# An SBUF offset: 128 bytes left free at the right end, and the S5 decays moved out of the constants

## The chip, the cores and the metric

The kernel runs on one core of a Trainium2 chip. The metric is the device time of one execution in microseconds (us). Before the change three runs gave 2323.28, 2323.66 and 2326.3 us, so the median is 2323.66 us. The profile was taken from one further execution, which has its own time.

The engines are named as in the profile: PE is the matrix engine, PEld its loading of the stationary operand, DVE the vector engine, ACT the scalar engine, POOL is GpSimd, SP issues most of the transfers. SBUF is the on-chip memory from which PE reads both of its operands; an address in it is a byte offset within each of 128 partitions.

## The reference

A residual trunk of two layers on 1024 positions of width 1024, all in float32. Layer 0 mixes positions with an S5 state-space mixer and a gated linear unit, layer 1 with a gated short convolution. Each mixer is followed by a dense feed-forward network (FFN) of hidden width 2816 and by a gated per-layer embedding (PLE). Cut to what matters:

```python
for i in range(DEPTH):
    hn = rmsnorm(h, norm_mix_g[i])
    mix = s5_mixer(hn, ...) if i % 2 == 0 else shortconv_mixer(hn, ...)
    h = h + mix
    h = h + swiglu_ffn(rmsnorm(h, norm_ffn_g[i]), ffn_w_in[i], ffn_w_out[i])
    gate = sigmoid(rmsnorm(h, norm_ple_g[i]) @ ple_w_gate[i])
    h = h + gate * (p[i] @ ple_w_up[i])
return rmsnorm(h, final_norm_g)
```

## The kernel before

**How a product is made.** Every float32 matrix operand is split into two float32r parts, a high and a low one (`split`, L86: a cast on ACT, L87, and a subtraction on DVE, L88). `mm3` (L121) then adds three products into PSUM: high times high (L122), high times low (L123), low times high (L124). Each is one PE matmul with a stationary operand of 128 partitions by 128 columns and a moving operand of 128 by 512. PE loads a stationary operand anew for each of them. The program has 8712 such full-width matmuls behind the S5 part's own small ones, and they run in long rows one behind another.

**Where the operands lie.** A stack of pools grows from the left end of SBUF and another from the right end. On the left lie the constants (pool `const`), then `ulow` (the activations, or room for weights), the residual `h`, and the pools of the stage: `ws` (weights of the input products), `w8` (shown as `w`, weights of the output products). On the right lie `rawp` (four buffers of 4 KB for what transfers bring in, `raw`; the hidden activations come in there under the name `ch`) and, behind the S5 part, `uhigh` (48 KB, activations or weights). Inside these tiles every matmul operand begins at a multiple of 512 bytes from the tile's start. So an operand's address modulo 512 is that of its tile.

**Which pairs PE reads.** The profile writes a matmul as out<-moving,stationary. Seven pairs make up the full-width float32r products behind the S5 part:

| moving, stationary | stage | matmuls | ends of SBUF |
|---|---|---|---|
| ulow, ws | input products of both FFNs and the convolution | 2688 | left, left |
| uhigh, ws | the same stages | 2016 | right, left |
| ulow, ch | output products of both FFNs and the convolution | 1344 | left, right |
| w, ch | the same | 576 | left, right |
| uhigh, ch | output products of both FFNs | 576 | right, right |
| uhigh, ulow | half of the gated linear unit and of each PLE gate | 768 | right, left |
| w, ulow | the other half | 744 | left, left |

The input products use a seven-product block scheme (`block_product`): of its seven products the first four read `ulow`, the last three `uhigh`, always against `ws`. The output products run in groups of hidden tiles whose weights lie in `ulow`, `uhigh` or `w8`, always with `ch` as the stationary operand.

**What sets the order.** The program is written engine by engine through a scheduler that takes the order of the text, priorities and a model of times; each engine then runs its own list in order. The S5 part's decay table `r8` (256 bytes per partition) is read by the scan on DVE (L981, L982) and by nothing else.

Of the kernel before, what the change touches and what calls it, by code (L numbers as in the profile page):

```python
# [9 lines left out]
F32 = mybir.dt.float32  # L10
# [7 lines left out]

P = 128
MAGIC = 12582912.0  # L20


@with_exitstack
def trunk(
# [17 lines left out]
    NG, NP = s5_a_re.shape[1], s5_a_re.shape[2]  # L42
# [5 lines left out]
    const = ctx.enter_context(tc.tile_pool(name="const", bufs=1))  # L48
# [562 lines left out]
    for tl, v in ((sgnA, 1.0), (sgnN, -1.0)):  # L611
        V.memset(tl[R0], v)
        V.memset(tl[R1], -v)
    r8 = const.tile([P, NG], F32, name="r8")
    rstd = const.tile([P, T], F32, name="rstd")

    rawp = ctx.enter_context(tc.tile_pool(name="rawp", bufs=1, side="right"))
    gen = tc.alloc_tile_pool(name="s5g", bufs=1, side="right")
    st = tc.alloc_tile_pool(name="s5t", bufs=1, side="right")

    def small(shape=(P, NG), dt=F32):
        return st.tile(list(shape), dt, name="sm", tag="sm", bufs=28)

    def ts(o, a, s1, op0, s2=None, op1=None):
        if op1 is None:
            V.tensor_scalar(o, a, s1, None, op0)
        else:
            V.tensor_scalar(o, a, s1, s2, op0, op1)
        return o
# [5 lines left out]
    def stt(o, a, s, b, op0, op1):  # L635
        V.scalar_tensor_tensor(o, a, s, b, op0, op1)
        return o

    def exp_to(o, a, shape):
        n = small(shape)  # L640
        ts(n, a, 1.4426950408889634, ALU.mult, MAGIC, ALU.add)
        ts(n, n, -MAGIC, ALU.add, 129.0, ALU.min)
        ts(n, n, -127.0, ALU.max)
# [86 lines left out]
    kq = small()  # L730
    ts(kq, ang, 2.0 / math.pi, ALU.mult, MAGIC, ALU.add)
    ts(kq, kq, -MAGIC, ALU.add)
    r = small()
# [3 lines left out]
    m4 = small()  # L737
    ts(m4, kq, 0.25, ALU.mult, MAGIC, ALU.add)
    ts(m4, m4, -MAGIC, ALU.add)
    stt(m4, m4, -4.0, kq, ALU.mult, ALU.add)  # L740
# [423 lines left out]
```

## Time and profile before

| | us |
|---|---|
| median of three runs | 2323.66 |
| the profiled execution | 2323.06 |
| its span, first to last instruction | 2321.3 |
| PE busy (matmuls) | 2240.0 (96% of the span) |
| PE loading stationary operands | 1832.0 (79%) |
| DVE busy | 1331.0 (57%) |
| ACT busy | 765.3 (33%) |
| POOL busy | 161.8 (7%) |

How to read it: a matmul's record lasts longer than its turn on PE, since one begins while the one before still drains. The record of a full-width matmul is some 0.39 us long, while the next one starts 0.23 us after it. So the pace of PE is read from the distance between starts, which the timeline gives, and not from the mean length of a record. The page's chain of waits gives PE 91% of the span; the mean granted clock of PE is 0.987 of the full one.

### The profile page before, as it was taken

What the parts mean: (1) busy time and instruction counts of PE and PEld (TensorE: products, weight loads), DVE (VectorE), ACT (ScalarE), POOL (GpSimd) and SP (SyncE); (2) the same over time, 40 slices, a digit from 0 to 9 for tenths busy, and PEclk for the clock granted to TensorE, in tenths of its full rate; (3) what the DMA queues carried; (4) which work ended last, traced back from release to release, by engine and by line L of the source; (5) the groups of instructions that cost most, each with busy time, mean ns of one, the idle gap of its engine ahead of it and who ended that gap; (6) DMA issues with size and microseconds to landing.
All of it is one profiled execution on the core that took longest, in us unless ns stands there. A gap on an engine that the chain in (4) does not pass through costs nothing.

```text
span 2321.3 us, 27094 instructions
## 1 busy us (share of the span) xinstructions
PE 2240.0 (96%) x10253; PEld 1832.0 (79%) x10253; DVE 1331.0 (57%) x2244; ACT 765.3 (33%) x1449; POOL 161.8 (7%) x268
## 2 busy tenths in 40 slices
PE   6987999899999999999989999979999999999998
PEld 5776887688888888888868888868888888888887
DVE  7885325866666642224488776486666666222444
ACT  6554223433333320013343332253333333100232
POOL 2110001000000000000010000010000000000000
PEclk9999999999999999999989999989999999999999
DMA  7656201333333365433232234544333334643323
GB/s 245 149 138 150 70 19 69 103 109 109 109 109 109 109 227 181 149 119 114 89 111 84 92 94 152 192 131 118 109 109 109 109 109 141 231 163 123 127 87 109
DMA packets 212978, 288.87 MB, mean 124 GB/s; under 512 B 21360, under 2 KB 152432, under 8 KB 212848
## 3 DMA queue, kind: packets, MB, share of 16 engines
q1 hardware_dynamic: 191520, 212.63, 29.3%
q0 software_dynamic: 20928, 74.47, 10.4%
q8 instruction: 80, 1.31, 0.2%
q14 instruction: 50, 0.41, 0.1%
q10 hardware_dynamic: 400, 0.04, 0.0%
HBM read 190.93 MB, written 79.69 MB: 117 GB/s over the span
## 4 chain that ended last, share of the span: by engine, by line
PE 91%; DVE 4%; DMA 3%; ACT 1%; SPq 1%; issue 1%; POOL 0%; DVEq 0%; POOLq 0%; ACTq 0%
PE psmm L122 29%; PE psmm L124 29%; PE psmm L123 29%; PE pstr L185 1%; PE pstr L997 1%; DVE W L632 1%; DMA raw<-in_ffn_w_in_dram 1%; PE pstr L998 0%; PE pstr L999 0%; PE pstr L931 0%; DMA tw<-tmp 0%; DVE gv L982 0%; DVE tmp L632 0%; DVE xn L177 0%; PE pstu L122 0%
## 5 line engine op out<-in xcount | busy, mean ns | idle before, releaser
L122 PE MATMUL psmm<-ulow,ws 128*128 128x512 f32 x896 | 351.8, 394 | 5.7 <-ACT ws L87 3.1
L123 PE MATMUL psmm<-ulow,ws 128*128 128x512 f32 x896 | 351.5, 393 | 2.5 <-DVE ulow L88 2.5
L124 PE MATMUL psmm<-ulow,ws 128*128 128x512 f32 x896 | 351.4, 393 | 2.0 <-DVE ws L88 2.0
L124 PE MATMUL psmm<-uhigh,ws 128*128 128x512 f32 x672 | 265.3, 395 | 0.0
L122 PE MATMUL psmm<-uhigh,ws 128*128 128x512 f32 x672 | 265.0, 395 | 0.0
L123 PE MATMUL psmm<-uhigh,ws 128*128 128x512 f32 x672 | 264.9, 394 | 0.0
L409 DVE TENSOR_TENSOR h<-psmm,h 128x512 f32<-128x512 f32 x128 | 88.3, 690 | 234.4 <-PE psmm L124 234.4
L88 DVE TENSOR_TENSOR ws<-raw,ws 128x512 fp32r<-128x512 f32 x224 | 153.6, 688 | 115.1 <-ACT ws L87 115.0
L87 ACT CAST ws<-raw 128x512 fp32r<-128x512 f32 x224 | 137.8, 619 | 208.7 <-PE psmm L124 201.9
L122 PEld LDWEIGHTS psmm<-ulow,ws 128*128 128x128 f32 x896 | 169.6, 189 | 43.6 <-ACT ws L87 4.2
L123 PEld LDWEIGHTS psmm<-ulow,ws 128*128 128x128 f32 x896 | 169.6, 189 | 39.7 <-DVE ulow L88 3.5
L124 PEld LDWEIGHTS psmm<-ulow,ws 128*128 128x128 f32 x896 | 169.5, 189 | 39.1 <-DVE ws L88 3.0
L123 PE MATMUL psmm<-ulow,ch 128*128 128x512 f32 x448 | 177.2, 396 | 0.0
L122 PE MATMUL psmm<-ulow,ch 128*128 128x512 f32 x448 | 176.9, 395 | 0.0
L124 PE MATMUL psmm<-ulow,ch 128*128 128x512 f32 x448 | 176.9, 395 | 0.0
L87 ACT CAST ws<-st 128x512 fp32r<-128x512 f32 x168 | 104.2, 620 | 211.9 <-PE psmm L124 192.1
L123 PEld LDWEIGHTS psmm<-uhigh,ws 128*128 128x128 f32 x672 | 126.2, 188 | 30.3
L124 PEld LDWEIGHTS psmm<-uhigh,ws 128*128 128x128 f32 x672 | 126.1, 188 | 30.3
L122 PEld LDWEIGHTS psmm<-uhigh,ws 128*128 128x128 f32 x672 | 126.2, 188 | 29.0
L370 POOL DMA_DIRECT2D hid<-hs x104 | 78.1, 754 | 917.6 <-DVE hs L88 908.7
L140 ACT ACTIVATE junk<-h 128x512 bf16<-128x512 f32 (+1 forms) x113 | 64.1, 567 | 207.6 <-DVE h L409 122.8
L88 DVE TENSOR_TENSOR ws<-st,ws 128x512 fp32r<-128x512 f32 x168 | 115.2, 686 | 1.3 <-ACT ws L87 1.2
(241 smaller groups left out, 3997.9 us busy)
## 6 DMA issues: line engine op xcount, KB each, us to landing
hid<-hs POOLq DMA_DIRECT2D x104, 512.0 KB, 4.3
ch<-hid SPq DMA_DIRECT2D x96, 512.0 KB, 3.8
raw<-in_ffn_w_in_dram SPq DMA_DIRECT2D x88, 512.0 KB, 4.4
raw<-in_ffn_w_out_dram SPq DMA_DIRECT2D x44, 512.0 KB, 4.0
hd<-h POOLq DMA_DIRECT2D x24, 512.0 KB, 2.9
h<-hd SPq DMA_DIRECT2D x24, 512.0 KB, 5.8
raw<-in_conv_w_in_dram SPq DMA_DIRECT2D x24, 512.0 KB, 3.9
up<-ev SPq DMA_DIRECT2D x32, 256.0 KB, 3.2
```

Source lines behind the costliest of these rows:

```text
L87: A.copy(hi, src)
L88: V.tensor_tensor(lo, src, hi.bitcast(F32), ALU.subtract)
L122: PE.matmul(ps, ahi, bhi, start=start, stop=False, skip_group_check=more)
L123: PE.matmul(ps, ahi, blo, start=False, stop=False, skip_group_check=more)
L124: PE.matmul(ps, alo, bhi, start=False, stop=stop, skip_group_check=more)
L140: done["square"] = A.activation(junk[:, cs], h[t][:, cs], AF.Square, scale=1.0 / math.sqrt(D), accum_out=ms).ins
L185: PE.transpose(pt[:, c * P:(c + 1) * P], xn[:, kt * P:(kt + 1) * P], ident)
L370: nc.gpsimd.dma_start(out=hid[ht // 4][half * HT:(half + 1) * HT, :, ht % 4].rearrange("t p l j -> p t l j"), in_=hs.bitcast(F32))
L409: done["sum"] = V.tensor_tensor(h[t][:, cs], ps[nb], h[t][:, cs], ALU.add).ins
L632: V.tensor_tensor(o, a, b, op)
L997: PE.matmul(o, Us[b][:, g, :], Ms[b][:, g, :], start=True, stop=False)
```

## The change

No instruction is added, removed or moved: every engine's list, with its waits, is the same as before, name for name. Only addresses change. A tile of 32 float32 words (128 bytes per partition) is laid at the right end of SBUF and never written or read, so everything on the right begins 128 bytes lower. And `r8` leaves the constants at the left end for the S5 part's own pool on the right, so everything to the left that lies behind the constants begins 256 bytes lower.

```diff
+EDGE = 32
...
-    r8 = const.tile([P, NG], F32, name="r8")
     rstd = const.tile([P, T], F32, name="rstd")
 
+    edge = ctx.enter_context(tc.tile_pool(name="edge", bufs=1, side="right"))
+    edge.tile([P, EDGE], F32, name="edge")
     rawp = ctx.enter_context(tc.tile_pool(name="rawp", bufs=1, side="right"))
     gen = tc.alloc_tile_pool(name="s5g", bufs=1, side="right")
+    r8 = gen.tile([P, NG], F32, name="r8")
     st = tc.alloc_tile_pool(name="s5t", bufs=1, side="right")
```

What the built programs give as the tiles' first bytes:

| tile | end | before | modulo 512 | after | modulo 512 |
|---|---|---|---|---|---|
| ulow | left | 18016 | 96 | 17760 | 352 |
| ws, first buffer | left | 83552 | 96 | 83296 | 352 |
| w (w8), first buffer | left | 116320 | 96 | 116064 | 352 |
| uhigh | right | 163808 | 480 | 163680 | 352 |
| raw and ch, first buffer | right | 212960 | 480 | 212832 | 352 |
| ws, end of the last buffer | left | 128608 | | 128352 | |
| w, end of the last buffer | left | 149088 | | 148832 | |
| r8 | | 17632 | 224 | 174688 | 96 |
| ident (transposes) | left | 16512 | 128 | 16512 | 128 |

Before, a left and a right tile differ by 128 (or 384) modulo 512; after, by nothing. Modulo 128 no full-width matmul operand moves.

## The prediction

> **What bounds the kernel now.** I began with the page: busy time by engine, then the chain of work that ended last.
>
> ```profile
> PE 2240.0 (96%) x10253; PEld 1832.0 (79%) x10253; DVE 1331.0 (57%) x2244; ACT 765.3 (33%) x1449; POOL 161.8 (7%) x268
> ...
> PE 91%; DVE 4%; DMA 3%; ACT 1%; SPq 1%; issue 1%; POOL 0%; DVEq 0%; POOLq 0%; ACTq 0%
> ```
>
> PE is busy nearly always, and 91% of the chain is its own. Whether it is short of work inside a stage is seen in the busy time by stretches; the columns are the stretch, its length, busy us and count for PE, PEld, DVE, ACT and POOL, then the granted clock, the DMA share and GB/s.
>
> ```profile
> 400.00:500.00 100.00, 90.88 (x394) 73.11 (x393) 78.58 (x135) 43.89 (x80) 6.53 (x10) 0.95 0.36 108
> ...
> 500.00:800.00 300.00, 300.00 (x1308) 245.26 (x1307) 197.73 (x312) 108.12 (x188) 23.95 (x32) 1.00 0.39 112
> 860.00:1080.00 220.00, 220.00 (x970) 179.14 (x969) 62.53 (x84) 30.40 (x49) 3.27 (x6) 1.00 0.43 146
> 1300.00:1400.00 100.00, 100.00 (x437) 81.72 (x436) 73.39 (x111) 33.62 (x54) 7.76 (x16) 1.00 0.31 96
> 1600.00:1900.00 300.00, 300.00 (x1308) 245.08 (x1307) 197.72 (x311) 107.03 (x187) 22.46 (x30) 1.00 0.38 109
> 2000.00:2180.00 180.00, 180.00 (x789) 146.60 (x788) 47.38 (x60) 21.98 (x31) 1.10 (x2) 1.00 0.44 150
> ```
>
> Inside the FFN and convolution stages PE never stops: 300.00 of 300.00 us, at the full clock. The next engine, DVE, has work for 197.73 us of 300. Idle time stands at the borders of stages, as in the first row, where the clock falls too. So in the stages the time is the number of matmuls times the distance between two starts, and I looked next at whether this distance is the same for all pairs of operands. First the numbers of matmuls, from the groups kept apart by shape (one of the three lines of `mm3` each, out<-moving,stationary, then busy us and the mean ns of a record):
>
> ```profile
> L122 PE MATMUL psmm<-ulow,ws 128*128 128x512 f32 x896 | 351.8, 394 | 5.7 <-ACT ws L87 3.1 <-ACT ulow L87 1.9 <-ACT s L348 0.7
> L122 PE MATMUL psmm<-uhigh,ws 128*128 128x512 f32 x672 | 265.0, 395 | 0.0
> L122 PE MATMUL psmm<-ulow,ch 128*128 128x512 f32 x448 | 176.9, 395 | 0.0
> L122 PE MATMUL psmm<-uhigh,ulow 128*128 128x512 f32 x256 | 100.9, 397 | 0.6 <-ACT uhigh L87 0.6
> L122 PE MATMUL psmm<-w,ch 128*128 128x512 f32 x192 | 76.2, 397 | 0.0
> L122 PE MATMUL psmm<-uhigh,ch 128*128 128x512 f32 x192 | 74.8, 390 | 0.0
> ```
>
> The records' means differ little. The starts, from PE's timeline, differ more. For each pair I show the first and the last row of a stretch within one run of that pair, on the same line of `mm3`; the first column is the start in us.
>
> ```profile
> 1707.44 0.39 PE L124 MATMUL psmm<-ulow,ws 128*128 128x512 f32 x1
> ...
> 1714.24 0.39 PE L124 MATMUL psmm<-ulow,ws 128*128 128x512 f32 x1
> 1714.46 0.40 PE L122 MATMUL psmm<-uhigh,ws 128*128 128x512 f32 x1
> ...
> 1719.36 0.39 PE L122 MATMUL psmm<-uhigh,ws 128*128 128x512 f32 x1
> ```
> ```profile
> 2000.04 0.39 PE L124 MATMUL psmm<-ulow,ch 128*128 128x512 f32 x1
> ...
> 2012.64 0.39 PE L124 MATMUL psmm<-ulow,ch 128*128 128x512 f32 x1
> ```
> ```profile
> 1000.58 0.39 PE L122 MATMUL psmm<-uhigh,ch 128*128 128x512 f32 x1
> ...
> 1005.34 0.39 PE L122 MATMUL psmm<-uhigh,ch 128*128 128x512 f32 x1
> ```
> ```profile
> 300.57 0.39 PE L122 MATMUL psmm<-w,ulow 128*128 128x512 f32 x1
> ...
> 307.37 0.39 PE L122 MATMUL psmm<-w,ulow 128*128 128x512 f32 x1
> ```
> ```profile
> 2189.98 0.39 PE L122 MATMUL psmm<-w,ch 128*128 128x512 f32 x1
> ...
> 2191.38 0.39 PE L122 MATMUL psmm<-ulow,ch 128*128 128x512 f32 x1
> ```
> ```profile
> 2231.16 0.39 PE L124 MATMUL psmm<-uhigh,ulow 128*128 128x512 f32 x1
> ...
> 2234.64 0.39 PE L124 MATMUL psmm<-uhigh,ulow 128*128 128x512 f32 x1
> ```
>
> With the matmuls in between counted:
> - both operands at one end: ulow,ws 6.80 us / 30 = 226.7 ns; uhigh,ch 4.76 / 21 = 226.7; w,ulow 6.80 / 30 = 226.7.
> - one operand at each end: uhigh,ws 4.90 / 21 = 233.3; ulow,ch 12.60 / 54 = 233.3; w,ch 1.40 / 6 = 233.3; uhigh,ulow 3.48 / 15 = 232.0.
>
> All of it at clock 1.00, and the first two stretches follow each other within 12 us. The pairs of one end start at one offset modulo 512 (96 and 96, or 480 and 480), those of two ends do not (96 and 480). Neither the tile, nor its role as moving or stationary operand, nor the stage sorts them: uhigh is fast against ch and slow against ws, ulow fast against ws and slow against ch.
>
> **The change, part by part.** No instruction comes, goes or moves, and no wait; so no queue and no wait is passed by another, and only what an address does to a duration can change.
>
> *The full-width products.* After the change all seven pairs begin at 352, so each should step as the pairs of one end do now. The offset 352 itself has no row; 96 and 480, which differ in both address bits that the change moves, have the same 226.7 ns, so I take that. Matmuls of both ends are three times the rows' counts:
> - uhigh,ws 3 × 672 = 2016, by 6.6 ns: 13.3 us
> - ulow,ch 3 × 448 = 1344, by 6.6: 8.9 us
> - w,ch 3 × 192 = 576, by 6.6: 3.8 us
> - uhigh,ulow 3 × 256 = 768, by 5.3: 4.1 us
>
> That is 30.1 us. All of it lies on the path, since PE is full in these stages.
>
> *What is taken off.* A faster PE asks its suppliers sooner: the FFN's input stages give DVE 300 / 1.013 = 296 us for the same 198 us of work, which is still far from full. ACT and DVE wait for PE there, not the other way about, as the waits by engine say (us in total, times, the longest):
>
> ```profile
> ACT ws L87 <- PE psmm L124: 394.0, 216, 4.0
> DVE h L409 <- PE psmm L124: 234.4, 108, 7.5
> PE psmm L122 <- ACT ws L87: 3.1, 3, 1.3
> ```
>
> At the starts of stages PE waits for chains of DVE, ACT and transfers that keep their length. There some products of two ends run while PE is not the bound. If at each of six borders it is one block's 36, that is 36 × 6.6 ns = 0.24 us, 1.4 us in all; if it is all of them in 100 us around it (436 × 3/7 = 187, 1.2 us), 7.4 us. I take 1.5, since the waits that end PE's idle time are few and short in the row above, and keep 0 and 7.
>
> *The other engines.* ACT, DVE and the transfers read and write the shifted tiles too. The nearest rows are the subtraction in `split`, with its two SBUF inputs at two offsets (raw at 480, ws at 96) and at one (st and ws, both at 96):
>
> ```profile
> L88 DVE TENSOR_TENSOR ws<-raw,ws 128x512 fp32r<-128x512 f32 x224 | 153.6, 688 | 115.1 <-ACT ws L87 115.0
> L88 DVE TENSOR_TENSOR ws<-st,ws 128x512 fp32r<-128x512 f32 x168 | 115.2, 686 | 1.3 <-ACT ws L87 1.2
> ```
>
> 2 ns in 688, and behind PE's work. I take nothing; if DVE's 4% of the chain (93 us, mostly the S5 part) moved by that share, it would be 0.3 us either way. The transposes against ident, which begins at 128, have two offsets before (480 or 96) and after (352).
>
> ```profile
> L185 PE MATMUL pstr<-ident,xn 128*128 128x128 f32 x264 | 37.7, 284 | 12.7 <-DVE xn L177 12.7
> L963 PE MATMUL pb<-U,wbt 128*128 128x128 f32 x128 | 17.3, 286 | 2.2 <-ACT wbt L914 2.2
> ```
>
> The S5 part's product U,wbt (left and right) becomes a pair of one offset; at the same 3% (6.6 of 226.7) its 17.3 us would give 0.5 us, and the transposes' 37.7 us could lose or gain 1.1 us. I take zero for both, with ±1.6 us.
>
> *A change of pair.* The first three steps of a one-end run behind a two-end run are longer, 0.69 us / 3 = 230 ns:
>
> ```profile
> 1720.06 0.39 PE L122 MATMUL psmm<-ulow,ws 128*128 128x512 f32 x1
> ...
> 1720.75 0.39 PE L122 MATMUL psmm<-ulow,ws 128*128 128x512 f32 x1
> ```
>
> If that is the delay of the run ahead being caught up, it goes too: 3 × 3.3 = 10 ns, once in each of the 56 blocks of the input stages (2688 / 48) 0.6 us, and with the output stages at most some 2 us. I leave it out of the sum and in the range.
>
> *Sum.* 30.1 − 1.5 = 28.6 us. The profiled execution's 2323.06 us (span 2321.3 and 1.8 around it) becomes 2294.5; it stands 0.6 us below the median of the runs, so the forecast for the median is 2295 us, 1.2% less.
>
> **A rule against it.** The rows say that two reads by PE disturb each other by some 6.6 ns a matmul according to their addresses. The Trainium skill, "SBUF — State Buffer", section "Who interferes with whom", says the contrary: PE has two read ports, one for the moving operand and one for loading the stationary one, independent of each other, and PE never waits on anyone; by it an address could not matter, and the time would stay at 2323.7. The trace disagrees, with 233.3 against 226.7 ns under one clock; the time that the rule gives is the second rival's, and its chance is in that one.
>
> **The rivals.**
> 1. *The gain is eaten by the suppliers.* In the input stages PE would meet transfers and DVE earlier. For it: DVE is at 73.39 of 100 us in the convolution (1300:1400). Against: it is not at 100 anywhere in the rows. If the gain of uhigh,ws were all lost, 13.3 us, the time is 2308.
> 2. *It is the end of SBUF, not the offset.* In the trace the two always go together: every slow pair has one operand at each end. Then nothing changes, and the change does not do what its words say: 2323.7. Against it: distance does not sort the pairs, since ulow (from 18016) with w (up to 149088) is fast though they lie up to 131 KB apart, while uhigh (from 163808) and the last ws buffer (up to 128608) are slow 35 KB apart; a border that does it would have to lie just between 149088 and 163808.
> 3. *Slower: PE, now denser, loses clock.* The mechanism is the granted clock in the stages with PE full, 8712 × 226.7 ns = 1975 us. The gain is gone where 1975 × (1/c − 1) = 28.6, at c = 0.986; at 0.97 it costs 61 us and the time is 2295 + 61 = 2356. Against it: the clock is 1.00 in every row with PE full, those with runs of 226.7 ns steps among them, and falls only where PE stops (0.95 in 400:500).
>
> **How the numbers follow.** Forecast 0.82: 2295 us; with the terms left open (0 to 7 us at the borders of stages, ±1.6 us for S5 and transposes, up to 2 us at changes of pair) 2290 to 2302. First rival 0.09, second 0.06, third 0.03. The range is 2289 to 2303, which takes in the smaller losses of the first rival; outside are the rest of it and the other two. A measurement of this kernel can tell 0.2%, 4.6 us, from no change: the forecast and the first rival are faster by more, 0.91; the second is the same, 0.06; slower 0.03.
>
> **What would show it.** Right: PE's starts in uhigh,ws and ulow,ch at 226.7 ns like ulow,ws, all records of these groups near 390 ns, DVE's and ACT's mean times unchanged, FFN input stages shorter by some 5.2 us each (792 × 6.6 ns), their output stages by 5.1 (768 × 6.6). Wrong: pairs of two ends still at 233 ns (second rival); 226.7 ns reached, but rows of PE with less than 300 of 300 us (first); a clock below 1.00 where PE is full (third); or all pairs at some other step, if 352 is not like 96 and 480.

## The result, and the profile after

The changed kernel takes 2295.32 us (median of four runs, 2293.48 to 2295.71) against 2324.06 us (median of four runs, one more than ahead of the prediction): a ratio of 0.9873, 95% interval 0.9856 to 0.989. Its profiled execution takes 2295.08 us with a span of 2293.3, 28.0 us less than before in both. Timed a second time, beside other runs of the kernel before, the ratio was 0.9878 (0.9862 to 0.9895).

The page after the change: busy time by engine, then the chain.

```profile
PE 2212.2 (96%) x10253; PEld 1831.3 (80%) x10253; DVE 1330.9 (58%) x2244; ACT 765.5 (33%) x1449; POOL 162.4 (7%) x268
...
PE 91%; DVE 4%; DMA 3%; SPq 1%; ACT 1%; issue 0%; POOL 0%; DVEq 0%; POOLq 0%; ACTq 0%
```

PE is busy 27.8 us less for the same 10253 records; DVE, ACT and the loading of stationary operands keep their times. The groups by shape (line numbers of the helpers, `mm3` among them, are one higher than before):

```profile
L123 PE MATMUL psmm<-ulow,ws 128*128 128x512 f32 x896 | 352.3, 394 | 5.9 <-ACT ws L88 3.1 <-ACT ulow L88 2.0 <-ACT s L349 0.7
L123 PE MATMUL psmm<-uhigh,ws 128*128 128x512 f32 x672 | 261.2, 389 | 0.0
L123 PE MATMUL psmm<-ulow,ch 128*128 128x512 f32 x448 | 174.5, 389 | 0.0
L123 PE MATMUL psmm<-uhigh,ulow 128*128 128x512 f32 x256 | 99.5, 391 | 0.6 <-ACT uhigh L88 0.6
L123 PE MATMUL psmm<-w,ch 128*128 128x512 f32 x192 | 75.3, 392 | 0.0
```

The records of the pairs of two ends are now 389 to 392 ns long on this line instead of 395 to 397; ulow,ws stays at 394. The pace is read from the starts again. The first rows of the next fence, from PE's timeline, are the first and the last of a run of `uhigh,ws`; the others belong to the first group of output products of the second FFN, one run of 384 matmuls.

```profile
1695.75 0.39 PE L123 MATMUL psmm<-uhigh,ws 128*128 128x512 f32 x1
...
1700.51 0.39 PE L123 MATMUL psmm<-uhigh,ws 128*128 128x512 f32 x1
...
1951.43 0.39 PE L123 MATMUL psmm<-ulow,ch 128*128 128x512 f32 x1
...
2038.24 0.39 PE L125 MATMUL psmm<-ulow,ch 128*128 128x512 f32 x1
```

That is 4.76 us / 21 = 226.7 ns and 86.81 / 383 = 226.7 ns, where it was 233.3 for both pairs. The clock and the fill of PE in the stages, in the columns of the prediction's stretches:

```profile
500.00:800.00 300.00, 300.00 (x1325) 248.43 (x1324) 200.07 (x315) 108.97 (x189) 24.01 (x32) 1.00 0.39 111
1580.00:1880.00 300.00, 300.00 (x1325) 248.42 (x1324) 199.45 (x315) 108.24 (x188) 23.34 (x32) 1.00 0.39 112
```

PE is still full, still at clock 1.00, and does 1325 matmuls in 300 us instead of 1308.

Where the 28.0 us come from, by the first start of each stage's products in the two timelines (us from one stage's first full-width product to the next one's, in the last row to its own last one):

| stage | before | after | less |
|---|---|---|---|
| S5 part, up to the first product behind it | 221.7 | 222.2 | −0.5 |
| gated linear unit | 188.1 | 185.7 | 2.4 |
| FFN input, layer 0 | 434.0 | 430.1 | 3.9 |
| FFN output, layer 0 | 248.7 | 243.9 | 4.8 |
| PLE, layer 0 | 105.8 | 104.9 | 0.9 |
| convolution input | 233.8 | 230.9 | 2.9 |
| convolution output | 115.1 | 112.0 | 3.1 |
| FFN input, layer 1 | 426.5 | 421.8 | 4.7 |
| FFN output, layer 1 | 248.6 | 243.8 | 4.8 |
| PLE, layer 1 | 85.2 | 84.3 | 0.9 |

All stages with these products gain, and the S5 part ahead of them does not.

### The profile page after: what moved, and what is told of

Same layout as the page of the kernel before. It is cut to its first block, busy times and chain, and to the rows that moved or that the text cites. A ratio compares the mean times of both kernels' runs of the same rounds, so it can differ in the third digit from the quotient of the medians.

```text
span 2293.3 us, 27094 instructions
## 1 busy us (share of the span) xinstructions
PE 2212.2 (96%) x10253; PEld 1831.3 (80%) x10253; DVE 1330.9 (58%) x2244; ACT 765.5 (33%) x1449; POOL 162.4 (7%) x268
## 4 chain that ended last, share of the span: by engine, by line
PE 91%; DVE 4%; DMA 3%; SPq 1%; ACT 1%; issue 0%; POOL 0%; DVEq 0%; POOLq 0%; ACTq 0%
PE psmm L123 29%; PE psmm L125 29%; PE psmm L124 29%; PE pstr L186 1%; DVE gv L985 1%; PE pstr L1000 1%; DVE W L635 1%; PE pstr L1001 1%; PE pstr L1002 1%; DMA tw<-tmp 0%; DMA raw<-in_ffn_w_in_dram 0%; PE pstr L934 0%; DMA W<-W 0%; DVE tmp L635 0%; DMA h<-in_x_dram 0%
## 5 line engine op out<-in xcount | busy, mean ns | idle before, releaser
L124 PE MATMUL psmm<-uhigh,ws 128*128 128x512 f32 x672 | 261.4, 389 | 0.0
L123 PE MATMUL psmm<-uhigh,ws 128*128 128x512 f32 x672 | 261.2, 389 | 0.0
L125 PE MATMUL psmm<-uhigh,ws 128*128 128x512 f32 x672 | 261.2, 389 | 0.0
L124 PE MATMUL psmm<-ulow,ch 128*128 128x512 f32 x448 | 174.6, 390 | 0.0
L123 PE MATMUL psmm<-ulow,ch 128*128 128x512 f32 x448 | 174.5, 389 | 0.0
L125 PE MATMUL psmm<-ulow,ch 128*128 128x512 f32 x448 | 174.3, 389 | 0.0
```

Source lines behind the costliest of these rows:

```text
L123: PE.matmul(ps, ahi, bhi, start=start, stop=False, skip_group_check=more)
L124: PE.matmul(ps, ahi, blo, start=False, stop=False, skip_group_check=more)
L125: PE.matmul(ps, alo, bhi, start=False, stop=stop, skip_group_check=more)
```

## The experiments

A prediction that comes out right may still be right for another reason. The rival reasons were that one end's own place or offset helps and not that both agree; that the region of SBUF decides; and that the distance has to vanish modulo something other than 512. In the table at the end of this section, "steps" are the mean distances between starts of successive full-width products, from the whole timeline, stops over 300 ns left out: first where the address of the moving operand and that of the next stationary one differ by a multiple of 256, then all others.

**Only the free bytes at the right end.** The decays stay in the constants:

```diff
-    r8 = gen.tile([P, NG], F32, name="r8")
...
+    r8 = const.tile([P, NG], F32, name="r8")
     rstd = const.tile([P, T], F32, name="rstd")
```

> Only the free 128 bytes at the right end; r8 stays in the constants. Left tiles begin at 96 modulo 512, right ones at 352: the two ends differ by 256. My theory (PE's step depends on whether its two operands begin at one offset modulo 512): pairs of two ends step at about 233 ns as before, the time is 2324 us (2318 to 2330; 256 has not been seen yet). Rival (the offset 352 of the right-hand tiles is what helps, or a lower right end): half or all of the gain, 2295 to 2310 us.

Measured: 2293.07 us, ratio 0.9864 (0.985 to 0.9879), as much as the whole change gives. Here the expectation of my theory failed. From PE's timeline, the first and the last of 384 matmuls `ulow,ch` of the first FFN's output, moving operand at 96, stationary at 352:

```profile
836.30 0.39 PE L123 MATMUL psmm<-ulow,ch 128*128 128x512 f32 x1
...
923.12 0.39 PE L125 MATMUL psmm<-ulow,ch 128*128 128x512 f32 x1
```

86.82 us / 383 = 226.7 ns. Two offsets that differ by 256 are as good as two equal ones: over the whole run, 3944 steps with a distance of 0 modulo 512 have a mean of 226.8 ns, and 4648 with 256 also 226.8.

**Only the decays moved.** Nothing is left free at the right end:

```diff
-    edge = ctx.enter_context(tc.tile_pool(name="edge", bufs=1, side="right"))
-    edge.tile([P, EDGE], F32, name="edge")
```

> Only r8 out of the constants, nothing left free at the right end. Left tiles begin at 352, right ones at 480: they differ by 128, as before by 384. My theory: steps of 233 ns for pairs of two ends and 226.7 for pairs of one, 2324 us (2320 to 2328). Rival (the left tiles' own offset 352 is what helps): 2295 to 2310 us.

Measured: 2323.66 us, ratio 0.9995 (0.9985 to 1.0004): no change. The same run of `ulow,ch`, 352 against 480:

```profile
843.09 0.40 PE L123 MATMUL psmm<-ulow,ch 128*128 128x512 f32 x1
...
932.46 0.39 PE L125 MATMUL psmm<-ulow,ch 128*128 128x512 f32 x1
```

89.37 us / 383 = 233.3 ns. So the left end's offset of 352 is worth nothing by itself. With the run before it, two explanations are left: that right-hand tiles at 352 are fast by themselves, or that the distance counts modulo 256.

**The left end split.** In the changed kernel, 128 free bytes above `ulow`:

```diff
+    gap = ctx.enter_context(tc.tile_pool(name="gap", bufs=1))
+    gap.tile([P, 32], F32, name="gap")
     hpool = tc.alloc_tile_pool(name="hp0", bufs=1)
```

> The changed kernel with 128 free bytes between ulow and what lies above it on the left: ulow and all right-hand tiles begin at 352, h, ws and w at 480. Now pairs of one end differ (ulow,ws 2688; w,ulow 744) and pairs of two ends with ulow do not (ulow,ch; uhigh,ulow); uhigh,ws 2016 and w,ch 576 differ. My theory: 6024 matmuls step at 232.8 instead of 226.8 ns, 36 us more than the changed kernel, 2331 us (2326 to 2337). Rival (the end of SBUF, or the region, decides and not the offset): ulow,ws and w,ulow stay at 226.7 ns; with uhigh,ws and w,ch slow or not, 2295 to 2311 us.

Measured: 2330.1 us, ratio 1.002 (1.001 to 1.0029), 0.9 us from the forecast. The timeline, first a run of 192 matmuls `w,ulow` (both on the left, 128 apart), then the 384 of `ulow,ch` (left and right, at one offset):

```profile
266.61 0.40 PE L125 MATMUL psmm<-w,ulow 128*128 128x512 f32 x1
...
311.17 0.39 PE L127 MATMUL psmm<-w,ulow 128*128 128x512 f32 x1
...
851.42 0.40 PE L125 MATMUL psmm<-ulow,ch 128*128 128x512 f32 x1
...
938.27 0.39 PE L127 MATMUL psmm<-ulow,ch 128*128 128x512 f32 x1
```

44.56 us / 191 = 233.3 ns within one end, 86.85 / 383 = 226.8 ns across the two. It is the reverse of the kernel before, with the right-hand tiles left where the change puts them. `uhigh,ws`, whose right-hand tile is still at 352, steps by 232.7 ns now that its left-hand one lies at 480. Neither the end, nor the region, nor the right end's 352 decides.

**Both ends at 256.** The S5 part's `rstd`, `sgnA` and `sgnN` go to its pool too, and the free space grows to 224 bytes:

```diff
-EDGE = 32
+EDGE = 56
...
-    sgnA = const.tile([P, 1], F32, name="sgnA")
-    sgnN = const.tile([P, 1], F32, name="sgnN")
-    rstd = const.tile([P, T], F32, name="rstd")
...
+    rstd = gen.tile([P, T], F32, name="rstd")
+    sgnA = gen.tile([P, 1], F32, name="sgnA")
+    sgnN = gen.tile([P, 1], F32, name="sgnN")
```

> The changed kernel with rstd, sgnA and sgnN in the S5 part's pool and 224 free bytes at the right end: both ends begin at 256 modulo 512. My theory (equality alone matters): all steps at 226.7 ns, 2295 us (2292 to 2298). Rival (what is left over the 213 ns that 512 columns would take at 2.4 columns per ns, an estimate, comes from the common offset 352 not being a multiple of 64 or 256): steps below 226.7 ns; if 5 ns go, 8712 x 5 = 44 us, 2251 us.

Measured: 2290.46 us, ratio 0.9851 (0.9836 to 0.9865); 8589 steps with a mean of 226.7 ns. The rival falls: a common offset that is a multiple of 256 steps like 96, 352 or 480. The 4.9 us below the changed kernel lie almost wholly ahead of the first product behind the S5 part, which starts at 217.9 us instead of 222.2. To see whether that stays, the changed kernel and this one ran once more side by side:

> The changed kernel once more, beside the next, to tell whether 352 or 256 as the common offset makes a difference: 2295 us (2293 to 2296).

> Both ends at 256 modulo 512, timed once more beside the changed kernel. Theory (full-width products do not care about the common offset, their steps were 226.7 and 226.8 ns): the same as the changed kernel within 0.1%, 2293 to 2296 us, and the 2290.5 of the first look was chance in the S5 part. Rival (the S5 part gains from the offset): 2290.5 again, with all of the difference ahead of the first product of the gated linear unit.

Measured: 2294.53 us (2293.71 to 2297.22) and 2292.77 us (2289.3 to 2293.57), ratios 0.9878 (0.9862 to 0.9895) and 0.9864 (0.9849 to 0.9879). The S5 part now ended at 221.3 and 220.0 us. The second lies 0.2 us below its forecast, but the intervals overlap; a gain in the S5 part of a tenth of a per cent isn't excluded and isn't shown.

**Other distances.** The changed kernel with 192 free bytes, then with 160:

```diff
-EDGE = 32
+EDGE = 48
```
```diff
-EDGE = 32
+EDGE = 40
```

With the decays left in the constants neither of the two has room: the pool `t2a` (10 KB per partition) then lacks 64 or 32 bytes.

> The changed kernel with 192 instead of 128 free bytes at the right end: left tiles at 352, right ones at 288 modulo 512, 64 apart. The runs so far have 0 and 256 apart at 226.8 ns a step and 128 or 384 apart at 232.8. Theory A (what counts is the distance modulo 256, and any other than 0 costs the same): pairs of two ends at about 233 ns, 2324 us. Theory B (modulo 64 would do, and 128 is a special bad distance): 226.8 ns, 2294 us. Theory C (the cost grows with the distance, 0 at 0 and 6 ns at 128): 229.8 ns, 2294 + 4648 x 3 ns = 2308 us.

> The same with 160 free bytes: left tiles at 352, right ones at 320, 32 apart. Theory A: about 233 ns, 2324 us. Theory B: 226.8 ns, 2294 us. Theory C: 226.8 + 6 x 32/128 = 228.3 ns, 2294 + 4648 x 1.5 ns = 2301 us.

Measured: 2321.76 us, ratio 0.999 (0.9981 to 1.0), and 2326.68 us, ratio 1.0013 (1.0003 to 1.0023). From the timeline at 32 apart, the 384 matmuls `ulow,ch` again:

```profile
843.98 0.39 PE L123 MATMUL psmm<-ulow,ch 128*128 128x512 f32 x1
...
933.34 0.39 PE L125 MATMUL psmm<-ulow,ch 128*128 128x512 f32 x1
```

89.36 us / 383 = 233.3 ns. Thirty-two bytes apart cost as much as 128, so the theories B and C fall and A holds.

At 64 apart A holds only in part. Where the moving operand begins 64 below the stationary one (`uhigh,ws`, `uhigh,ulow`), the mean of 2759 steps is 233.3 ns. Where it begins 64 above (`ulow,ch`, `w,ch`), the mean of 1887 steps is 230.1, and this is a mixture. The 384 matmuls `ulow,ch` of the first FFN read the same addresses in the same order as the 384 of the second, at clock 1.00 in both. The first two rows are from the second to the last matmul of the first FFN's run, the other two are the whole run of the second FFN:

```profile
845.81 0.39 PE L124 MATMUL psmm<-ulow,ch 128*128 128x512 f32 x1
...
933.25 0.39 PE L125 MATMUL psmm<-ulow,ch 128*128 128x512 f32 x1
...
1972.35 0.40 PE L123 MATMUL psmm<-ulow,ch 128*128 128x512 f32 x1
...
2061.72 0.40 PE L125 MATMUL psmm<-ulow,ch 128*128 128x512 f32 x1
```

That is 87.44 us / 382 = 228.9 ns and 89.37 us / 383 = 233.3 ns. So at this distance the addresses alone do not fix the pace. The other runs of these two pairs, as far as they have more than 12 matmuls, step by 228.8 to 229.3 ns; what picks between the two paces stays open.

All of it together:

| kernel | left | right | us | steps, multiple of 256 apart | steps, other |
|---|---|---|---|---|---|
| before | 96 | 480 | 2324.06 | 227.3 (3959) | 232.8 (4648) |
| changed | 352 | 352 | 2295.32 | 226.8 (8590) | none |
| only the free bytes | 96 | 352 | 2293.07 | 226.8 (8592) | none |
| only the decays | 352 | 480 | 2323.66 | 227.3 (3949) | 232.8 (4648) |
| left end split | 352 and 480 | 352 | 2330.1 | 227.2 (2659) | 232.8 (5935) |
| both at 256 | 256 | 256 | 2290.46 | 226.7 (8589) | none |
| 64 apart | 352 | 288 | 2321.76 | 227.6 (3956) | 232.0 (4646) |
| 32 apart | 352 | 320 | 2326.68 | 227.7 (3951) | 233.4 (4648) |

## Why the prediction was right, and where it was not

*PE's starts bound the stages.* Right. Every stage with full-width products is shorter, and PE is as full as before.

*Pairs of two ends fall from 233.3 to 226.7 ns.* The fall came, but the term was too large: 4648 steps went from a mean of 232.84 to 226.80 ns, which is 28.1 us where the sum had 30.1. The prediction took the 233.3 ns of a few long stretches for whole pairs, while many runs outside the longest step by 232.0 to 232.7. By pairs the fall is 6.2 ns for `uhigh,ws`, 6.4 for `ulow,ch` and 5.3 to 5.5 for `w,ch` and `uhigh,ulow`.

*A change of pair.* Right, and it should have been in the sum. Before, the first three steps of `ulow,ws` behind a run of `uhigh,ws` took 231.7, 232.5 and 230.9 ns in the mean; after, they take 226.6 to 226.7 like the others. All steps of one-end pairs went from 227.33 to 226.80 ns, 3959 × 0.53 = 2.1 us, the upper of the two figures given.

*What is taken off.* 1.5 us were taken; the timelines give 1.7. Before, 104 steps over 300 ns sum to 103.6 us, after, 121 sum to 109.1; less 226.8 ns for each, that is 80.0 and 81.7 us. The FFN input stages show it most: stops take back 1.5 of 5.4 us in layer 0 and 0.8 of 5.5 us in layer 1, so these stages gain 3.9 and 4.7 us, where 5.2 were forecast. The FFN output stages gain 4.8 of the 5.1 forecast.

Together 28.1 + 2.1 − 1.7 − 0.5 (the S5 part) = 28.0 us, as measured; the forecast was 28.6. That it came so near is in part luck: a term 2.0 us too large stands against one of 2.1 us that was left out.

*The other engines.* Right: the subtraction of `split` has the same means as before, with its input at 352 as at 480. The S5 part, with its transposes, takes 222.2 us, and 221.3 when run again, against 221.7 before; no gain or loss shows.

```profile
L89 DVE TENSOR_TENSOR ws<-raw,ws 128x512 fp32r<-128x512 f32 x224 | 153.6, 688 | 113.3 <-ACT ws L88 113.2
L89 DVE TENSOR_TENSOR ws<-st,ws 128x512 fp32r<-128x512 f32 x168 | 115.2, 686 | 1.2 <-ACT ws L88 1.1
```

*One offset modulo 512.* The step that failed. The prediction took the modulus from the numbers 96 and 480, with which 128, 256 and 512 were not all told apart: their distance, 384, is 128 modulo 256 and nothing modulo 128. So modulo 128 was excluded by the trace of before, and 256 was not. The runs show 256, and with it that the move of `r8` was not needed: the free bytes alone give the whole gain.

*The rivals.* The end of SBUF as the cause is excluded by the split left end (233.3 ns within one end, 226.8 across). The suppliers took back no more than the 1.7 us of stops; the clock stayed at 1.00. The Trainium skill's "SBUF — State Buffer", section "Who interferes with whom", by which PE's two read ports are independent and PE never waits on anyone, does not account for the pace of these products: 232.8 to 233.4 ns against 226.8 by nothing but an address.

*Still open.* The runs show that the pace depends on the two operands' addresses; that the two reads get in each other's way is a reading of this, not shown. The records of PE's loads do not hold the lost time: before the change their means are 187.7 to 188.3 ns for the slow pairs and 187.7 to 189.3 for the fast ones. Which read waits, if one does, where the period of 256 bytes comes from, and why 64 bytes apart has two paces was not told apart: in each run every product of a pair has both its operands at the pair's offsets.

## What to carry to other kernels

Where PE is full and loads a stationary operand for each matmul, compare the distance between starts by pairs of operands, not only the mean record; a pair that is slower everywhere, whatever its stage and neighbours, points to its addresses. For products like these (float32r, 128 by 128 by 512, a load before each) let all tiles that PE reads together begin at one offset modulo 256, across both ends of SBUF. The 128 bytes of padding at one end did it here, and 128 bytes between two left-hand tiles undid it. Check the modulus with a second distance before more than the padding is moved; here that would have spared the move of `r8`.

## What was not expected of the hardware

- The period of 256 bytes: at distances 0 and 256 a float32r product of 128 by 128 by 512 steps by 226.8 ns, and at 32, 128 and 384 by 232.8 to 233.4 ns. Of whole periods only 0 and 256 were tried.
- Thirty-two bytes apart cost as much as 128; less than 32 was not tried.
- At 64 apart a run of 384 products took 228.9 ns a step and another, with the same addresses and the same clock, 233.3.
- No layout stepped faster than 226.7 ns. The Trainium skill, "TensorE: Matmul & The Clock Gate", section "Wait — 56ns, not 53.3ns?", gives 215.7 ns start to start for 512 columns at the full clock; no run here reaches that, and what the other 11 ns are was not tried.
